# Sixteen projection units as seven block products each, ahead of both attentions, with their results kept in DRAM

## The chip, the cores and the metric

The kernel runs on one core of a Trainium2 chip. The metric is the device time of one execution in microseconds, as the median of several runs. The engines are TensorE (PE in the profile; its weight loads are PEld), VectorE (DVE), ScalarE (ACT), GpSimd (POOL) and SyncE (SP), which issues nearly all DMAs.

## What is computed

One pre-norm layer on x of 1024 tokens x 1024 channels, in float32. Cut to what matters here:

```python
h = rms_norm(x, g)
proj = h @ w_in                    # 1024 x 11280, split into
# c_val, c_gate | g_q, g_k, g_v, g_og, g_f | d_q, d_k, d_v | m_conv, m_gla, m_diff
o_conv = silu(layer_norm(causal_conv31(c_val * sigmoid(c_gate)))) @ w_conv_out
o_gla  = rms_norm(gla(g_q, g_k, g_v, g_f)) * silu(g_og)      # 4 heads, scan over chunks
o_diff = rms_norm(diff_attention(d_q, d_k, d_v)) * 0.8       # 8 heads, two softmaxes each
y = sigmoid(m_conv) * o_conv + sigmoid(m_gla) * o_gla + sigmoid(m_diff) * o_diff
x = x + y @ w_out
x = x + swiglu(rms_norm(x)) @ w_ffn_out                      # FFN of 2816 hidden channels
out = rms_norm(x)
```

## The kernel before

Every float32 matrix product is made of three matmuls in the reduced format: each operand is split into a high and a low half (`hilo`, lines 110 to 112: the cast on ScalarE, the difference on VectorE), and `mm3` (114 to 117) adds high x high, high x low and low x high in PSUM. All weights come as units of 256 output columns (two loads of 512 KB by `raw_half`, four pieces split by `operand`), one unit ahead of their use.

A unit is used by `proj_t` (four outputs of 128 channels x 512 tokens, each over 8 k-tiles: 96 matmuls of 512 columns) or by `proj_n` (tokens on partitions: 192 matmuls of 256 columns, for V and DV). The FFN input product (units FG and FU) is different: it cuts the 256 x 1024 weights and the 1024 x 1024 activations into 2 x 2 blocks and needs seven block products in place of eight (Strassen's scheme in Winograd's form). The block sums of the activations, T1 to T4, are made once; those of the weights (`lefts`, four per unit) and the sums of the products (`copy` on ScalarE, `finish` on VectorE) come in every unit.

`units()` lists the units in order, and the program is written out by a clock of ticks: each `yield` of a projection is a tick, twelve to a unit. On a tick the next weight piece is issued on every second one, convolution taps at a rate of 0.95 per tick (`taps`; each tap is one VectorE instruction over 128 x 1024, `conv_taps`), and every generator that is due (`spawn`, `resume`). For the GLA part the units of a head are CV, A (q and k), V, CV, OG (output gate) and MG (the merge gate); the state scan of the head (`gla_core`, one step for each 128 tokens) and its output (`gla_out`) run among the units that follow. For the attention part they are DV, QK, MD (merge gate), QK for two heads; the softmaxes and value products (`diff_core`) run among the units, spaced by `SPACE` and `LAG` in ticks. Then come MG of the last GLA head, four MC units, the pointwise product PW, the output product WO and the FFN.

Scores lie in PSUM tiles of two banks (`bank2`, two buffers); all else in single banks (`bank`, four buffers). The branch sums lie in y_d in DRAM: the GLA output is stored there, and an attention head loads it, adds its own part on VectorE and stores it again. The framework that builds the program orders the instructions of each engine by its own model of their times, so their order need not be that of the code.

## Time and profile before

| | before |
|---|---|
| median of 3 runs | 2097.28 us (2096.46 to 2097.86) |
| profiled execution | 2096.91 us, span 2095.1 us |
| TensorE busy | 2072.3 us (99%), 10988 matmuls |
| VectorE busy | 1361.4 us (65%) |
| ScalarE busy | 806.3 us (38%) |
| GpSimd busy | 45.5 us (2%) |
| moved by DMA | 196.54 MB, mean 94 GB/s |

The span runs from the first to the last instruction of the profiled execution; its time holds 1.8 us more. A busy share is the union of an engine's instructions; matmuls overlap, so a matmul's own duration is longer than its distance to the next one. In the list of what an engine waited for, the name on the right is the instruction that released it.

### The profile page before, as it was taken

Reading aid. Unit: us, or ns where it says so; the run is one execution under the profiler, and the core shown is the slowest. Engines: PE = TensorE matmul, PEld = TensorE weight load, DVE = VectorE, ACT = ScalarE, POOL = GpSimd, SP = SyncE. Lnnn points to the kernel's source line nnn. Section 1 sums busy time; section 2 is a strip of 40 time slices with the busy share of each in tenths; the row PEclk is TensorE's granted clock in tenths of the full one; section 3 lists DMA queues with packets and bytes.
Section 4 is the critical chain, followed back from the end, with each engine's and each line's share of the span. In section 5 each row is a group of like instructions: output and inputs, shape, how many; then the busy total and the mean of one; then the engine's idle time right before and its main releaser. Section 6 shows DMA issues by size and latency. Waiting matters only on the chain.

```text
span 2095.1 us, 28027 instructions
## 1 busy us (share of the span) xinstructions
PE 2072.3 (99%) x10988; PEld 1779.2 (85%) x10988; DVE 1361.4 (65%) x2056; ACT 806.3 (38%) x1649; POOL 45.5 (2%) x45
## 2 busy tenths in 40 slices
PE   8999999999999999999999999999999999999998
PEld 6988988988898988989888888997888888888886
DVE  5988898798774545545455564469555455577766
ACT  6343252251324545545455451235333333432112
POOL 0000000000000000000000000000000000000000
PEclk9999999999999999999999999999999999999999
DMA  4112112112133323233231555333222222282111
GB/s 161 37 64 77 51 41 81 57 43 72 51 96 86 91 71 106 66 89 92 72 106 61 201 176 170 111 141 119 93 81 98 73 76 96 90 292 89 53 41 81
DMA packets 76579, 196.54 MB, mean 94 GB/s; under 512 B 9024, under 2 KB 19904, under 8 KB 76448
## 3 DMA queue, kind: packets, MB, share of 16 engines
q1 hardware_dynamic: 76448, 194.76, 29.3%
q8 instruction: 86, 1.41, 0.3%
q14 instruction: 45, 0.37, 0.1%
HBM read 137.58 MB, written 38.27 MB: 84 GB/s over the span
## 4 chain that ended last, share of the span: by engine, by line
PE 95%; DVE 3%; issue 1%; POOL 1%; DMA 1%; ACT 0%; SPq 0%; DVEq 0%; POOLq 0%
PE pb L115 23%; PE pb L116 23%; PE pb L117 23%; PE sc L115 6%; PE sc L116 6%; PE sc L117 6%; PE pb L680 3%; PE sc L645 2%; PE sc L644 2%; PE pb L669 2%; POOL sm L122 1%; DVE wl L112 0%; DVE xn L1129 0%; PE pb L504 0%; PE pb L561 0%
## 5 line engine op out<-in xcount | busy, mean ns | idle before, releaser
L115 PE MATMUL pb<-h,wh 128*128 128x512 f32 x1152 | 457.7, 397 | 0.0
L117 PE MATMUL pb<-h,wl 128*128 128x512 f32 x1152 | 450.2, 391 | 0.0
L116 PE MATMUL pb<-h,wh 128*128 128x512 f32 x1152 | 449.9, 391 | 0.0
L111 ACT CAST wh<-wr 128x512 fp32r<-128x512 f32 x331 | 203.7, 622 | 402.5 <-DVE x L1121 139.3
L112 DVE TENSOR_TENSOR wl<-wr,wh 128x512 fp32r<-128x512 f32 x331 | 226.2, 687 | 161.3 <-ACT wh L111 158.5
L362 DVE SCALAR_TENSOR_TENSOR acc<-up,par,acc 128x1024 f32<-128x1024 f32 x240 | 307.0, 1279 | 2.7
L117 PEld LDWEIGHTS pb<-h,wl 128*128 128x128 f32 x1152 | 216.2, 188 | 46.5
L116 PEld LDWEIGHTS pb<-h,wh 128*128 128x128 f32 x1152 | 216.7, 188 | 41.6 <-DVE h L228 0.9
L115 PEld LDWEIGHTS pb<-h,wh 128*128 128x128 f32 x1152 | 216.6, 188 | 41.4 <-ACT h L227 0.3
L1121 DVE TENSOR_TENSOR x<-x,pb 128x512 f32<-128x512 f32 x176 | 120.2, 684 | 61.2 <-PE pb L117 60.6
L115 PE MATMUL pb<-wh,h 128*128 128x256 f32 x512 | 147.8, 289 | 0.0
L117 PE MATMUL pb<-wh,h 128*128 128x256 f32 x512 | 144.9, 283 | 0.0
L116 PE MATMUL pb<-wl,h 128*128 128x256 f32 x512 | 144.8, 283 | 0.0
L115 PE MATMUL sc<-bT,wh 128*128 128x512 f32 x352 | 137.0, 390 | 0.5 <-ACT bT L111 0.5
L116 PE MATMUL pb<-wl,mh 128*128 128x512 f32 x352 | 136.9, 389 | 0.0
L117 PE MATMUL pb<-wh,ml 128*128 128x512 f32 x352 | 136.9, 389 | 0.0
L115 PE MATMUL pb<-wh,mh 128*128 128x512 f32 x352 | 136.9, 389 | 0.0
L116 PE MATMUL sc<-bT,wh 128*128 128x512 f32 x352 | 136.8, 389 | 0.0
L117 PE MATMUL sc<-bT,wl 128*128 128x512 f32 x352 | 136.6, 389 | 0.0
L111 ACT CAST wh<-s 128x512 fp32r<-128x512 f32 x88 | 54.6, 621 | 129.6 <-PE sc L116 91.3
L116 PEld LDWEIGHTS pb<-wl,h 128*128 128x128 f32 x512 | 98.1, 192 | 0.2
L115 PEld LDWEIGHTS pb<-wh,h 128*128 128x128 f32 x512 | 98.1, 192 | 0.2
(242 smaller groups left out, 3663.2 us busy)
## 6 DMA issues: line engine op xcount, KB each, us to landing
wr<-w_dram SPq DMA_DIRECT2D x176, 512.0 KB, 3.7
m_d<-t SPq DMA_DIRECT2D x44, 256.0 KB, 2.1
mr<-m_d SPq DMA_DIRECT2D x22, 512.0 KB, 5.9
y_d<-y SPq DMA_DIRECT2D x28, 256.0 KB, 2.0
k<-k SPq DMA_DIRECT2D x48, 128.0 KB, 2.3
kl<-kl SPq DMA_DIRECT2D x48, 128.0 KB, 2.4
xt<-x_dram SPq DMA_DIRECT2D x8, 512.0 KB, 5.6
c_d<-acc SPq DMA_DIRECT2D x8, 512.0 KB, 2.6
```

Source lines behind the costliest of these rows:

```text
L111: act.copy(hi, src)
L112: vec.tensor_tensor(out=lo, in0=src, in1=f(hi), op=ALU.subtract)
L115: pe.matmul(o, ah, bh, start=start, stop=False, skip_group_check=more)
L116: pe.matmul(o, ah, bl, start=False, stop=False, skip_group_check=more)
L117: pe.matmul(o, al, bh, start=False, stop=stop, skip_group_check=more)
L122: pool.tensor_tensor(out=dst, in0=dst, in1=mhalf[:, 0:width], op=ALU.pow)
L362: vec.scalar_tensor_tensor(out=acc, in0=up[:, j:j + S], scalar=w, in1=acc, op0=ALU.mult, op1=ALU.add)
L644: pe.matmul(sc[i][:, c], a["q"][i][:, t], a["k"][i][:, c], start=True, stop=False)
L645: pe.matmul(sc[i][:, c], a["q"][i][:, t], a["kl"][i][:, c], start=False, stop=True)
L669: pe.transpose(pt[:, i * P:(i + 1) * P], pd[:, (g0 + i) * P:(g0 + i + 1) * P], ident)
L680: pe.matmul(ov[:, 0:P], parts[k // 4][:, c], a["v"][:, k, :], start=k == 0, stop=k == nk - 1)
L1121: vec.tensor_tensor(out=xx, in0=xx, in1=o, op=ALU.add)
```

## The change

Sixteen units (5 CV, 4 OG, 3 MG and 4 MD) move to the front of the list, behind CV 0 and CV 1, and are computed as the FFN input is, by seven block products over all 1024 tokens. The blocks of h are the existing tiles; T1 to T4 are made from them in the head, while CV 0 and CV 1 run. The class `Blocks` is the FFN's loop in a form that both stages use. Their results go to DRAM: the GLU output u to u_d (loaded again for the convolution, one channel tile ahead), the gates of GLA, already multiplied, to gt_d, and those of attention to dg_d; `gla_out` and `diff_core` load them back. The units of a GLA head that remain are A and V, those of two attention heads DV, QK and QK; CV 7 stands ahead of the first GLA head. The pool of the two attentions takes over the SBUF of the block stage when that is done, and the low-rank gate product is made then (`gla_begin`).

The taps have a rate by stage. A state step of GLA comes every two ticks, no longer three; the softmaxes come every two or three. The sums over convolution channels (s_d) and over branches (y_d, heads 0 to 5) are made by accumulating DMAs from GpSimd's queue. The scaling of osb and the factor dng move from VectorE to ScalarE.

```diff
-    out = []
+    out = [("CV", 0), ("CV", 1)]
     for h in range(NH):
-        out += [("CV", 2 * h), ("A", h), ("V", h), ("CV", 2 * h + 1), ("OG", h)]
-        if h < NH - 1:
-            out += [("MG", h)]
+        out += [("OG", h)] + [("MG", h)] * (h < NH - 1) + [("CV", 2 + h), ("MD", h)]
+    out += [("CV", 6)]
+    out += [("CV", 7)]
+    for h in range(NH):
+        out += [("A", h), ("V", h)]
     for j in range(ND // 2):
-        out += [("DV", j), ("QK", 2 * j), ("MD", j), ("QK", 2 * j + 1)]
+        out += [("QK", 2 * j), ("DV", j), ("QK", 2 * j + 1)]
     out += [("MG", NH - 1)] + [("MC", u) for u in range(4)]
...
-LAG = (3, 4, 3, 3, 4, 3, 5, 4)
-SPACE = (2, 2, 2, 3, 3, 4, 3, 3)
-SPACE_LAST = (1, 1, 2, 3, 2, 2, 5, 3)
+
+MIX0, MIX1 = 2, 18
+LAG = (3, 3, 3, 3, 4, 4, 4, 4)
+SPACE = (2, 2, 2, 2, 2, 2, 3, 3)
+TAP_RATE = {"head": 0.0, "blocks": 0.42, "gla": 0.5, "diff": 0.72}
...
+
+    conv = {"ready": deque(), "next": deque(), "now": None, "n": 0}
+    ups = [cv.tile([P, S + 32], F32, name=f"up{i}") for i in range(2)]
+
+    def conv_load():
+        while conv["ready"] and len(conv["next"]) + (conv["now"] is not None) < 2:
+            ct = conv["ready"].popleft()
+            up = ups[conv["n"] % 2]
+            conv["n"] += 1
+            sp.dma_start(up[:, TAPS - 1:TAPS - 1 + S], u_d[ct])
+            conv["next"].append((ct, up))
+
+    def conv_step():
+        if conv["now"] is None:
+            if not conv["next"]:
+                return False
+            conv["now"] = conv_taps(*conv["next"].popleft())
+        if next(conv["now"], None) is None:
+            conv["now"] = None
+        conv_load()
+        return True
+
     def taps(n):
         clock["conv"] = min(clock["conv"] + n, 2.0)
-        while clock["conv"] >= 1.0 and convq:
+        while clock["conv"] >= 1.0 and conv_step():
             clock["conv"] -= 1.0
-            if next(convq[0], None) is None:
...
-        taps(0.95)
+        taps(TAP_RATE.get(clock["stage"], 0.5))
...
+            if full is not None:
+                full[k] = x2_("hf")
+                act.activation(full[k], pt, AF.Copy, scale=g)
...
+        for name in ("T1", "T2", "T3", "T4"):
+            tblock(name)
+        for k in range(4):
+            a, b = full.pop(k), full.pop(k + 4)
+            old = lambda name, p: f(T[name][p][:, k, :])
+            put = lambda name, src: hilo(T[name][0][:, k, :], T[name][1][:, k, :], src)
+            t1, t2 = x2_("t1"), x2_("t2")
+            vec.tensor_tensor(out=t1, in0=a, in1=old("11", 0), op=ALU.subtract)
+            vec.tensor_tensor(out=t1, in0=t1, in1=old("11", 1), op=ALU.subtract)
+            put("T1", t1)
+            vec.tensor_tensor(out=t2, in0=b, in1=t1, op=ALU.subtract)
+            put("T2", t2)
+            yield 1
+            vec.tensor_tensor(out=b, in0=b, in1=a, op=ALU.subtract)
+            put("T3", b)
+            vec.tensor_tensor(out=t2, in0=old("21", 0), in1=t2, op=ALU.subtract)
+            vec.tensor_tensor(out=t2, in0=t2, in1=old("21", 1), op=ALU.add)
+            put("T4", t2)
+            yield 1
+        clock["stage"] = "blocks"
...
-    def conv_taps(ct, up, acc):
+    def conv_taps(ct, up):
+        acc = cv.tile([P, S], F32, tag="acc", name="acc", bufs=1)
...
         sp.dma_start(c_d[ct], acc)
         if ct == 0:
-            vec.tensor_copy(csum, acc)
+            sp.dma_start(s_d, acc)
         else:
-            vec.tensor_tensor(out=csum, in0=csum, in1=acc, op=ALU.add)
-        if ct == KT - 1:
-            sp.dma_start(s_d, csum)
+            pool.dma_start(s_d, acc, accum_op=ALU.add)
+        yield 1
+
+    def conv_in(ct, half, sg, o):
+
+        vec.scalar_tensor_tensor(out=sg, in0=sg, scalar=1.0, in1=o, op0=ALU.add, op1=ALU.mult)
+        sp.dma_start(u_d[ct][:, hs(half)], sg)
+
+    def conv_out(ct):
+        conv["ready"].append(ct)
+        conv_load()
...
+        if h + 1 < NH:
+            spawn(decay(h + 1), 2)
...
+        spawn(gla_core(h), 9)
...
-                yield 3 if pp else 6
+                yield 2
...
+                y = y2("gt")
+                sp.dma_start(y, gt_d[2 * h + v][:, hs(grp)])
+                yield 1
...
-        spawn(diff_core(h), 3)
+        spawn(diff_core(h), (9, 3)[h % 2])
...
-            at += (SPACE if h < ND - 1 else SPACE_LAST)[i]
+            at += SPACE[i]
...
-        vec.tensor_tensor(out=osb, in0=osb, in1=rs.unsqueeze(2).broadcast_to([P, NT, P]), op=ALU.mult)
+        for t in range(NT):
+            act.activation(osb[:, t, :], osb[:, t, :], AF.Copy, scale=rs[:, t:t + 1])
+        gts = [y2("dgate") for _ in range(2)]
+        for half in range(2):
+            sp.dma_start(gts[half], dg_d[h][:, hs(half)])
         yield 2
         for half in range(2):
             pt = bank()
             for t in range(4):
                 pe.transpose(pt[:, t * P:(t + 1) * P], osb[:, half * 4 + t, :], ident)
-            y = y2("y")
-            vec.scalar_tensor_tensor(out=y, in0=a["gate"][:, hs(half)], scalar=1.0, in1=pt, op0=ALU.add, op1=ALU.mult)
+            y = gts[half]
+            act.activation(pt, pt, AF.Copy, scale=dng)
+            vec.scalar_tensor_tensor(out=y, in0=y, scalar=1.0, in1=pt, op0=ALU.add, op1=ALU.mult)
             if h < 6:
-                yg = y2("yg")
-                sp.dma_start(yg, y_d[h, :, hs(half)])
-                vec.scalar_tensor_tensor(out=y, in0=y, scalar=dng, in1=yg, op0=ALU.mult, op1=ALU.add)
+                pool.dma_start(y_d[h][:, hs(half)], y, accum_op=ALU.add)
             else:
-                vec.tensor_scalar(out=y, in0=y, scalar1=dng, scalar2=None, op0=ALU.mult)
-            sp.dma_start(y_d[h, :, hs(half)], y)
+                sp.dma_start(y_d[h][:, hs(half)], y)
...
+    right = ("11", "T1", "T2", "21", "T3", "T4", "22")
+
+    def lefts(alloc, a11, a21, a12, a22):
+        s_ = {0: a11, 3: a12, 5: a22}
+        p = None
+
+        def comb(to, a, b, op):
+            s_[to] = like(alloc("s"), a11)
+            vec.tensor_tensor(out=s_[to], in0=a, in1=b, op=op)
+
+        while True:
+            p = yield operand(s_[p]) if p is not None else None
+            if p == 1:
+                comb(1, a21, a22, ALU.add)
+            elif p == 2:
+                comb(2, s_[1], a11, ALU.subtract)
+            elif p == 4:
+                comb(4, a11, a21, ALU.subtract)
+            elif p == 6:
+                comb(6, a12, s_[2], ALU.subtract)
...
+        def product(self, n, p):
+            if p == 0:
+                ab = bank2()
+                self.chain[n] = {"a": ab[:, 0:HALF], "b": ab[:, HALF:]}
+            ch = self.chain[n]
+            if p == 3:
+                ch["c"] = bank()
+            o = ch["abacaab"[p]]
+            wh, wl = self.made.pop((n, p))
+            bh, bl = self.blocks[right[p]]
+            fresh = p in (0, 1, 3)
+            for k in range(4):
+                kk = slice(k * P, (k + 1) * P)
+                mm3(o, wh[:, kk], wl[:, kk], bh[:, k, :], bl[:, k, :], fresh and k == 0, k == 3, not fresh)
+                if k % 2:
+                    tick()
+
+        def after(self, n, p):
+            ch = self.chain[n]
+            if p == 0:
+                ch["p1"] = self.copy(ch["a"])
+            elif p == 2:
+                ch["u2"] = self.copy(ch["a"])
+            elif p == 3:
+                self.finish(n, 0, 0, ch["p1"], ch["c"])
+            elif p == 4:
+                ch["u3"] = self.copy(ch["a"])
+                self.finish(n, 1, 1, ch["u3"], ch["b"])
+            elif p == 5:
+                self.finish(n, 1, 0, None, ch["a"])
+            elif p == 6:
+                self.finish(n, 0, 1, ch["u2"], ch["b"])
...
+    def mix_sums(n):
+        raws = [raw_half(MIX0 + n, hf) for hf in range(2)]
+        v = [r.rearrange("p (k c n) -> p c k n", k=4, c=2) for r in raws]
+        return lefts(xs2, v[0][:, 0], v[0][:, 1], v[1][:, 0], v[1][:, 1])
...
+    NM = MIX1 - MIX0
+    order = [(0, 0), (0, 3), (0, 1), (0, 2), (0, 4)]
+    for n in range(1, NM):
+        order += [(n, 0), (n - 1, 5), (n - 1, 6)] + [(n, p) for p in range(1, 5)]
+    order += [(NM - 1, 5), (NM - 1, 6)]
+    mb = Blocks(order, order, mix_sums, T, mix_finish, mix_copy)
...
+    w0 = unit()
+    run(conv_half(0, w0, 0))
+    w1 = unit()
+    run(conv_half(1, w1, 0))
+    run(conv_half(0, w0, 1))
+    conv_out(0)
+    for i, _ in enumerate(conv_half(1, w1, 1)):
+        tick()
+        if i % 2:
+            mb.make()
+    conv_out(1)
+    for n, p in order:
+        for _ in range(2):
+            if len(mb.made) < AHEAD:
+                mb.make()
+        mb.product(n, p)
+        if mb.nxt == len(order) and len(mb.made) < 4 and state["n"] == MIX0:
+            state["n"] = MIX1
+            wstart()
+        mb.after(n, p)
+    drain()
+    sx.release()
+    tp.release()
+    mix = tc.alloc_tile_pool(name="mix", bufs=1)
+    clock["stage"] = "gla"
+    spawn(gla_begin(), 0)
...
+    for kind, i in UNITS[MIX1:]:
         if kind not in mixing:
             break
-        if kind == "QK" and i == 1:
-            while convq:
-                taps(1)
+        if kind == "QK":
+            clock["stage"] = "diff"
+        if kind == "MG":
+            while conv_step():
+                pass
```

## Rows read from the trace of the kernel before

**Rows 1.** The page, busy time by engine and the granted clock in 40 slices.

```profile
PE 2072.3 (99%) x10988; PEld 1779.2 (85%) x10988; DVE 1361.4 (65%) x2056; ACT 806.3 (38%) x1649; POOL 45.5 (2%) x45
...
PEclk9999999999999999999999999999999999999999
```

**Rows 2.** Stretches: length, busy us (instructions) of PE, PEld, DVE, ACT, POOL, clock, DMA share.

```profile
50.00:600.00 550.00, 550.00 (x3035) 479.80 (x3034) 470.78 (x559) 195.85 (x373) 16.88 (x8) 1.00 0.18 57
600.00:1170.00 570.00, 570.00 (x3371) 503.14 (x3371) 289.62 (x542) 268.01 (x689) 13.08 (x8) 1.00 0.32 87
...
1440.00:1835.00 395.00, 394.48 (x1722) 321.15 (x1721) 225.00 (x351) 150.41 (x261) 0.00 (x0) 1.00 0.28 92
```

**Rows 3.** What TensorE waited for: us in total, times, longest us.

```profile
PE pb L225 <- DVE xt L287: 10.0, 5, 8.8
```

**Rows 4.** Timeline, TensorE in the pointwise product: start, duration, instruction.

```profile
1230.31 0.39 PE L115 MATMUL pb<-u,wh 128*128 128x512 f32 x1
...
1317.12 0.39 PE L117 MATMUL pb<-u,wl 128*128 128x512 f32 x1
```

**Rows 5.** Groups of instructions by shape: count, busy us, mean ns.

```profile
L362 DVE SCALAR_TENSOR_TENSOR acc<-up,par,acc 128x1024 f32<-128x1024 f32 x240 | 307.0, 1279 | 2.7
L112 DVE TENSOR_TENSOR wl<-s,wh 128x512 fp32r<-128x512 f32 x88 | 59.9, 684 | 25.6 <-ACT wh L111 25.5
L998 DVE TENSOR_TENSOR t<-sc,c 128x512 f32<-128x512 f32 x44 | 30.0, 683 | 2.1 <-PE sc L117 2.1
L953 DVE TENSOR_TENSOR s<-wr 128x512 f32<-128x512 f32 x42 | 28.9, 688 | 20.4 <-DMA wr<-w_dram 20.4
L382 DVE SCALAR_TENSOR_TENSOR up<-sg,pb 128x512 f32<-128x512 f32 x16 | 11.0, 687 | 17.5 <-PE pb L117 17.5
L488 DVE SCALAR_TENSOR_TENSOR gate<-sgm,gate 128x512 f32<-128x512 f32 x12 | 8.2, 680 | 0.0
L111 ACT CAST wh<-s 128x512 fp32r<-128x512 f32 x88 | 54.6, 621 | 129.6 <-PE sc L116 91.3 <-issue 14.5 <-PE pb L116 13.0
L1010 ACT COPY c<-sc 128x512 f32<-128x512 f32 x66 | 38.3, 580 | 11.1 <-PE sc L117 11.1
L348 ACT ACTIVATE sg<-pb 128x512 f32<-128x512 f32 x16 | 9.5, 594 | 54.1 <-PE pb L117 54.1
```

**Rows 6.** Busy time in one stretch of the GLA part (columns as in rows 2).

```profile
200.00:250.00 50.00, 50.00 (x328) 45.91 (x327) 49.52 (x55) 11.60 (x20) 0.00 (x0) 1.00 0.14 41
```

**Rows 7.** Chain that ended last, in order of time: first and fourth GLA head.

```profile
88.35 0.89 PE pb L504 x8
...
523.49 0.89 PE pb L504 x8
```

**Rows 8.** Timeline, one state step of GLA: its update matmul and its low half.

```profile
260.68 0.28 PE L115 MATMUL pb<-vh,knh 128*128 128x256 f32 x1
...
262.90 0.48 DVE L544 SCALAR_TENSOR_TENSOR ws<-zs,dec,ws 128x256 fp32r<-128x256 f32 x1 [1.18 <-ACT ws L543]
```

**Rows 9.** Chain that ended last: the same step of two attention heads, five heads apart.

```profile
666.68 0.89 PE pb L680 x8
...
996.82 0.89 PE pb L680 x8
```

**Rows 10.** DMA issues: count, KB each, median us to landing.

```profile
xt<-x_dram SPq DMA_DIRECT2D x8, 512.0 KB, 5.6
...
c_d<-acc SPq DMA_DIRECT2D x8, 512.0 KB, 2.6
```

**Rows 11.** What VectorE waited for: low halves 1440 to 1835, reciprocals whole span.

```profile
DVE wl L112 <- ACT wh L111: 107.0, 76, 2.1
...
DVE st L655 <- ACT sc L653: 69.7, 60, 2.6
```

**Rows 12.** Timeline, one softmax over 768 keys: first score matmul, last score read.

```profile
799.24 0.48 PE L644 MATMUL sc<-k,q 128*128 128x512 f32 x1
...
804.11 1.02 DVE L658 SCALAR_TENSOR_TENSOR p<-sc,st,p 128x768 f32<-128x768 f32 x1
```

More of the change, by code (lines that the diff above doesn't have):

```diff
@@ L173, in wk @@
         return tuple(p[:, k % 2 * 256 + c.start:k % 2 * 256 + c.stop] for p in w[k // 2])
-    events, clock = [], {"now": 0, "seq": 0, "conv": 0.0}
-    convq = deque()
+    events, clock = [], {"now": 0, "seq": 0, "conv": 0.0, "stage": "head"}
     def spawn(gen, after=0):
@@ L552, in gla_core @@
             yield 1
+        spawn(gla_out(h), 2)
     def gla_out(h):
@@ L611, in diff_v @@
             yield
-    def diff_m(j):
-        w = unit()
-        for c in range(2):
-            gt = g4("dgate")
-            A.setdefault(2 * j + c, {})["gate"] = gt
-            for half in range(2):
-                o = yield from proj_t(w, c, half, hset)
-                sigmoid2(gt[:, hs(half)], o)
-                yield
     def diff_core(h):
@@ new lines, in body, with __init__, make @@
+    class Blocks:
+        def __init__(self, order, makes, sums, blocks, finish, copy):
+            self.order, self.makes, self.nxt = order, makes, 0
+            self.sums, self.blocks, self.finish, self.copy = sums, blocks, finish, copy
+            self.gens, self.made, self.chain = {}, {}, {}
+        def make(self):
+            if self.nxt < len(self.makes):
+                n, p = self.makes[self.nxt]
+                self.nxt += 1
+                if n not in self.gens:
+                    self.gens[n] = self.sums(n)
+                    next(self.gens[n])
+                self.made[n, p] = self.gens[n].send(p)
+        def product(self, n, p):
[12 more added lines that the diff above has]
+                mm3(o, wh[:, kk], wl[:, kk], bh[:, k, :], bl[:, k, :], fresh and k == 0, k == 3, not fresh)
+                if k % 2:
+                    tick()
[14 more added lines that the diff above has]
+                self.finish(n, 0, 1, ch["u2"], ch["b"])
@@ L1046, in load_x3 @@
                 x3[t + i] = x[:, i, :]
+    fb = Blocks(order, makes, ffn_sums, B, finish, copy)
     for _ in range(4):
-        make()
+        fb.make()
     for at, (n, p) in enumerate(order):
```

310 lines of the change are left out of this document (137 added, 173 removed).

## The prediction, made before the change was run

> **What bounds the kernel now.** I read the page's totals first, then the busy time by stage, then what TensorE waited for, then single instructions. TensorE is busy 99% of the span at the full granted clock [rows 1]. By stage [rows 2] it is busy in all of 50 to 1170 us, where the sixteen units of this change now lie (GLA heads to about 600, attention heads after that); VectorE has 471 of 550 us there in the first part and 290 of 570 in the second. Of what TensorE ever waited for, the longest line is the start, 10.0 us [rows 3]; the few other lines are shorter than 2 us each and lie behind 1300. So in the changed stretch the only thing that ends late is TensorE's own list of matmuls, and a change is worth what it takes off that list, less the waits it makes.
>
> A busy TensorE is no proof of a full one, since matmuls overlap: one 128x512 matmul is shown with 390 ns, but the 384 matmuls of the pointwise product start at 1230.31 and the last of them at 1317.12 [rows 4], which is 86.81 / 383 = 0.2267 us from start to start. That is the price I use. The Trainium skill, "TensorE: Matmul & The Clock Gate", section "Back-to-back issue gap", gives about 131 ns for a sustained matmul of 512 columns; at that figure the saving would be, as an estimate, 192 x 0.131 = 25 us and the time 2080. The trace doesn't agree: 383 intervals in a row at 0.2267 us leave it no chance here.
>
> **Part 1: seven products for eight.** A unit of this shape is 8 k-tiles x 4 outputs x 3 matmuls = 96 matmuls of 512 columns; by block products it is 7 x 4 x 3 = 84. Units 2 to 17 are 5 CV, 4 OG, 3 MG and 4 MD: 16 x 12 = 192 matmuls fewer, 192 x 0.2267 = 43.5 us off TensorE. The FFN input runs the same scheme now: 1722 matmuls in 395 us [rows 2] is 0.2294 each, 0.0027 above the steady pace, while half a microsecond is shown as idle. The 1344 matmuls of the new stage at that pace cost 3.6 us back. Bounds 0 and 3.6; I take 3.6, the same loop.
>
> **Part 2: what the blocks cost VectorE and ScalarE.** Durations from [rows 5]. Per unit: 7 low halves and 4 sums at 0.69, 3 finishing additions at 0.68, the GLU product twice in CV at 0.69, the gate merge four times in MG at 0.68. Over 16 units 112 x 0.684 + 64 x 0.688 + 48 x 0.683 + 10 x 0.687 + 12 x 0.680 = 168.5 us. Taps: 224 ticks x 0.42 = 94 steps, of which 31 in 33 are multiplications, 88 x 1.279 = 113 us. Together 281 of the 308 us (1344 x 0.2294) that TensorE needs: 91%. ScalarE: 112 high halves at 0.62, 48 copies at 0.58 and 54 activations at 0.6 = 130 us, 42%. What hides this is that products are made up to seven ahead, 7 x 12 x 0.2267 = 19 us. That VectorE can run so full without TensorE waiting is shown: 200 to 250 us has VectorE at 49.52 and TensorE at 50.00 [rows 6]. Price 0; without cover it is the first rival.
>
> **Part 3: the head.** The low-rank product moves to the GLA stage (32 matmuls, 7 us, on TensorE either way). New are T1 to T4: 4 k-tiles x 10 VectorE instructions x 0.684 = 27.4 us and 16 high halves and 8 extra copies on ScalarE (about 15 us). They lie beside CV 0 and CV 1, 2 x 96 x 0.2267 = 43.5 us of TensorE, and no taps run there any more. Beside them VectorE has the eight low halves of the second half of h (6), four scalings of x (3), the second unit's weights and the first products' (about 7), four GLU products (2.7): some 46 us for 43.5 of cover, and the first T product is third in order. Bounds 0 and 10 (as long as the wait at the start [rows 3]); I take 3, near what is missing.
>
> **Part 4: GLA with A and V only.** A head now repeats every (523.49 - 88.35) / 3 = 145.0 us [rows 7]; without two CV, OG and MG it is 145.0 - 4 x 96 x 0.2267 = 58.0 us. These 24 ticks are 2.42 us each, and a state step comes every two ticks, 4.8 us (now three, 6.6). The state chain from the update matmul to the end of the low half is 260.68 to 263.38, 2.7 us [rows 8], so 2.1 us remain for VectorE's queue, one tap and a low half. VectorE has per head 145.0 x 471/550 = 124 us now, of which taps 79; less four units' weights (11), GLU, gate and csum work (8) 26 are left, plus 24 x 0.5 x 31/33 x 1.279 = 14.4: 40 of 58. Price 0, bounds 0 and 1 us for each of 28 steps.
>
> **Part 5: attention with QK and DV only.** A head repeats every (996.82 - 666.68) / 5 = 66.0 us [rows 9]; without half an MD unit 66.0 - 10.9 = 55.1, in 18 ticks of 3.06. VectorE: 290 x 66.0/570 = 33.5, less MD's two low halves (1.4), the scaling of osb (1.2, now eight ScalarE instructions) and the dng step (1.5, now in ScalarE and the DMA), plus 18 x 0.72 x 31/33 x 1.279 = 15.6 of taps: 45 of 55, 82%. ScalarE rises from 31 to about 33. Price 0; the second rival says where it ends.
>
> **Part 6: DRAM and the accumulating DMAs.** u, gates and dg go out and come back: some 25 MB more over 1000 us, where the DMA engines are busy 18 and 32% [rows 2]. The new loads and stores stand in SP's queue before weight loads, which are a unit ahead. The 19 accumulating DMAs are in POOL's queue, each waiting for a VectorE result; behind them stands the next head's rstd, with most of a head (55 us) to spare. The one accumulator tile is held by two DMAs before the next channel may start; the plain store takes 2.6 us and a load of this size 5.6 [rows 10], no accumulate is shown, and I bound it by 2.6 and twice 5.6. Two empty steps at 0.42 per tick are about 6 us, so at most 5 us of tap delay per channel, off TensorE's path. Price 0. Handing the SBUF of the block stage to the attention pool makes the GLA preparation wait for the last product, under CV 7's 22 us: 0 to 8, I take 2 (a load and a few copies could stick out).
>
> **The sum**, against the profiled execution's 2096.9 (span 2095.1; 0.4 below the median): 2096.9 - 43.5 + 3.6 + 3 + 2 = 2062.
>
> **Rivals.** First, VectorE becomes the pace. Its waits are not in the demand above: in the FFN low halves waited 107 us in 395 for ScalarE's high half [rows 11]; scaled to 308 us and halved that is 42, and 281 + 42 = 323 is 15 us over TensorE's 308. In attention each reciprocal waits for the exponentials, 69.7 us / 8 = 8.7 per head [rows 11], so 45 + 8.7 + 2 for other waits = 55.9 against 55.1, 6 us in eight heads. 2062 + 21 = 2083. For it: these waits are structural. Against: with taps in the queue they are filled, as in 200 to 250.
>
> Second, slower: the score buffers. For 5 key blocks and more a softmax holds both double banks, from its first score matmul to the last read of its scores: 799.24 to 805.13, 5.9 us [rows 12]. The next may begin after 2 ticks, 6.1 us, and needs the second bank 0.8 later: 6.9 us. Two such narrow places in each of 8 heads. If taps and weight halves stretch the chain to 10 us, the 16 places cost (10 - 6.9) x 16 = 50 us and TensorE, in order, gives the time to nobody: 2062 + 50 = 2112. It eats the whole gain from 6.9 + 35/16 = 9.1 us on. At 0.72 taps a tick 1.8 us are added on average, 7.7 us, which costs 13 us at most; so more than twice that would have to fall into the chain. Against it too: narrow places are followed by wide ones.
>
> Third, the change doesn't take the time it says: the 192 matmuls go, but the block loop, head, handover and the state steps stall near their upper bounds (3.6 + 10 + 8 + three quarters of 28 = 43 us): 2096, no change. That all come together speaks against it.
>
> **How the numbers follow.** Forecast 0.75 (2053 to 2075), VectorE as pace 0.13 (2075 to 2092), score buffers 0.08 (2093 to 2115), no change 0.04. Lowest is 2096.9 - 43.5 = 2053 with all costs at nothing; three below it for work that slides into the start's wait. From 2050 to 2088 holds eight in ten. A measurement of this kernel can tell 0.2%, 4 us: faster 0.86, same 0.05, slower 0.09.
>
> **What would show it.** Right: 84 matmuls per mixing unit starting 0.227 to 0.23 us apart, TensorE near 100% in all stages to the MC units, the attention heads 55 to 57 us apart, GLA heads 58 to 60, VectorE 80 to 95% throughout. Part 2 is wrong if low halves release TensorE in the block stage; part 3 if the first T product waits over 10 us; part 4 if ws releases TensorE, part 5 if score matmuls wait for the exponentials or for the p sum. A slower tap or a granted clock below 1 in the mixing stages would make the whole prediction wrong.

## The result, and the profile after

The changed kernel takes 2116.93 us (median of 4 runs, 2115.08 to 2118.91) against 2097.38 us in the same comparison: 1.0094 times as long, 95% interval 1.0076 to 1.0111. The forecast was 2062 with a range of 2050 to 2088. It was wrong, in sign too. The profiled execution has a span of 2113.3 us, 18.2 longer than before.

The page after, busy time by engine (answers [rows 1]):

```profile
PE 2048.8 (97%) x10796; PEld 1751.7 (83%) x10796; DVE 1447.5 (68%) x2218; ACT 892.8 (42%) x1843; POOL 60.8 (3%) x64
```

There are 192 matmuls fewer, as forecast, and TensorE is no longer busy all the time. The stretches of the kernel after: the first two are those of [rows 2], then the head, the blocks, the handover (the block buffers pass to the attention pool, and the low-rank gate product is made), the GLA heads and the attention heads, then two single slices (columns as in [rows 2]):

```profile
50.00:600.00 550.00, 526.55 (x2579) 442.02 (x2579) 500.95 (x641) 227.08 (x409) 12.62 (x9) 0.98 0.30 94
600.00:1170.00 570.00, 561.16 (x3577) 504.56 (x3577) 342.63 (x618) 312.32 (x822) 31.15 (x25) 1.00 0.36 94
...
0.00:60.00 60.00, 39.99 (x184) 32.02 (x185) 39.69 (x79) 35.01 (x61) 4.92 (x12) 0.97 0.36 135
60.00:375.00 315.00, 308.39 (x1333) 250.97 (x1333) 296.57 (x375) 127.19 (x219) 1.94 (x2) 0.99 0.33 106
375.00:430.00 55.00, 47.30 (x198) 36.65 (x197) 44.73 (x48) 18.58 (x28) 0.86 (x1) 0.94 0.37 105
430.00:700.00 270.00, 256.17 (x1642) 233.17 (x1642) 242.76 (x323) 117.48 (x250) 16.67 (x10) 0.97 0.26 80
700.00:1200.00 500.00, 495.85 (x3093) 442.33 (x3092) 255.52 (x507) 283.15 (x755) 25.93 (x22) 1.00 0.38 101
...
225.00:250.00 25.00, 22.10 (x97) 17.72 (x95) 20.44 (x26) 9.15 (x16) 1.07 (x1) 1.00 0.49 145
250.00:275.00 25.00, 24.62 (x101) 20.05 (x101) 23.78 (x29) 10.83 (x19) 0.00 (x0) 0.93 0.22 71
```

Before, TensorE had 550.00 of 550 in the first of these and the clock at 1.00. Now every stage has a hole, and the granted clock is under 1 in all of them but the attention heads.

To put a number on each stage I count what TensorE lost in it: the length of the stretch less the matmuls that start in it, each at its full-rate spacing from start to start, 0.2267 us for 512 columns [rows 4], and 0.175, 0.12 and 0.1115 for 384, 256 and 128 columns, read in the same way where they follow each other without a wait. The kernel before, whose TensorE is busy throughout from 60 us on, shows how exact that is: 0.6, 0.1, 1.2 and 3.4 us in the four later stages.

| stretch, us | lost before | lost after | more |
|---|---|---|---|
| head, 0 to 60 | 15.2 | 25.7 | 10.5 |
| blocks, 60 to 375 | 0.6 | 13.0 | 12.4 |
| handover, 375 to 430 | 0.1 | 10.6 | 10.5 |
| GLA heads, 430 to 700 | 1.2 | 23.1 | 21.9 |
| attention heads, 700 to 1200 | 3.4 | 10.5 | 7.1 |

Together 62.4 us more. The pointwise product, the first stage that the change leaves alone, starts at 1249.1 instead of 1230.3 [rows 4], 18.8 later, and behind it nothing differs (the FFN input still has its 1722 matmuls in 394.5 us). So the work in front of it shrank by 62.4 - 18.8 = 43.6 us, which is the 192 matmuls at 0.2267 us. This is bookkeeping and no second measurement of the saving, since the losses are counted at that same spacing; that the spacing still holds is shown where nothing waits (from 50 to 225 us TensorE loses under 0.6 us in any 25). More than all of the saving was lost again.

What TensorE waited for between 60 and 700 us, the three longest lines (us in total, times, longest us; before there is none in this stretch):

```profile
PE sc L125 <- DVE t L937: 6.6, 2, 3.3
PE pb L466 <- ACT wfx L457: 6.5, 1, 6.5
PE sc L125 <- ACT ah L121: 4.1, 1, 4.1
```

And VectorE, in the same stretch:

```profile
DVE acc L400 <- DMA s_d<-acc: 24.4, 5, 6.7
```

Line 400 is the first tap of a channel. It writes the one accumulator tile, and waits until the accumulating DMA of the previous channel has read it. The DMA issues (KB each, median us to landing; the plain store answers [rows 10]):

```profile
c_d<-acc SPq DMA_DIRECT2D x8, 512.0 KB, 3.1
...
s_d<-acc POOLq DMA_DIRECT2D x7, 512.0 KB, 8.2
```

The timeline at three places, the head, one change of channel, and the handover (start, duration, engine, line, instruction; in brackets the idle time ahead of it and what ended it):

```profile
12.07 2.42 ACT L121 CAST wh<-wr 128x512 fp32r<-128x512 f32 x4 [10.05 <-DMA wr<-w_dram]
14.39 1.05 ACT L323 ACTIVATE junk<-xt 128x1024 f32<-128x1024 f32 x1
...
17.20 1.12 PE L258 MATMUL pb<-cst,xt 128*128 128x128 f32 x4 [17.20 <-DVE sm L131]
...
233.30 1.07 POOL L408 DMA_DIRECT2D s_d<-acc  x1 [202.19 <-DVE acc L402]
237.15 0.69 DVE L122 TENSOR_TENSOR wl<-s,wh 128x512 fp32r<-128x512 f32 x1
241.53 0.75 DVE L400 TENSOR_SCALAR acc<-up,par 128x1024 f32<-128x1024 f32 x1 [3.69 <-DMA s_d<-acc]
...
249.64 0.69 DVE L937 TENSOR_TENSOR t<-sc,c 128x512 f32<-128x512 f32 x1
250.38 0.50 PE L125 MATMUL sc<-T,wh 128*128 128x512 f32 x1 [3.28 <-DVE t L937]
...
251.91 0.63 PE L125 MATMUL sc<-T,wh 128*128 128x512 f32 x1
252.34 0.63 PE L126 MATMUL sc<-T,wh 128*128 128x512 f32 x1
...
408.89 0.33 SPq L449 DMA_DIRECT2D wf<-wf_dram  x1
410.90 0.30 ACT L121 CAST wfx<-wf 128x128 fp32r<-128x128 f32 x1 [9.93 <-DMA wf<-wf_dram]
412.32 9.17 PE L466 MATMUL pb<-h,wfx 128*96 128x512 f32 x32 [6.54 <-ACT wfx L457]
```

Read the middle part first. GpSimd issues the accumulation at 233.30; VectorE comes to the next channel's first tap at 237.84 and stands 3.69 us. It works its queue in order, so the block finish t (line 937) comes only at 249.64, and the matmul that needs its PSUM bank starts 3.28 us late. Soon after, from 251.91 to 255.3 us, eight matmuls start about 0.43 us apart instead of 0.2267.

In the head, ScalarE's first work on data is now the cast of the first weights, for which it waits until 12.07; the squares of x, for which everything waits, stand behind it, and the first transposes start at 17.20 instead of 8.85. At the handover ScalarE waits 9.93 us for wf, whose load could only be issued once the block buffers were given back, and TensorE stands behind it with the low-rank product.

The chain of work that ended last shows the same stall on its way into a GLA head, and the same step of two attention heads, six heads apart (answers [rows 9]):

```profile
460.54 8.90 DMA s_d<-acc
469.52 0.76 DVE acc L400
...
473.39 1.14 DVE t L483
...
475.13 2.54 DVE t L486 x8
...
481.67 0.52 ACT ah L121
482.23 0.58 PE sc L125
...
756.68 0.89 PE pb L722 x8
...
1093.17 0.89 PE pb L722 x8
```

The accumulation holds VectorE to 469.5, the decay of the next head (483, 486) comes after it, ScalarE waits for that, and TensorE for ScalarE's ah: that is the 4.1 us of the list of waits. The attention heads follow each other every (1093.17 - 756.68) / 6 = 56.1 us, near the 55.1 of the forecast.

### The profile page after: what moved, and what is told of

Same layout as the page of the kernel before. It is cut to its first block, busy times and chain, and to the rows that moved or that the text cites. A ratio compares the mean times of both kernels' runs of the same rounds, so it can differ in the third digit from the quotient of the medians.

```text
span 2113.3 us, 28321 instructions
## 1 busy us (share of the span) xinstructions
PE 2048.8 (97%) x10796; PEld 1751.7 (83%) x10796; DVE 1447.5 (68%) x2218; ACT 892.8 (42%) x1843; POOL 60.8 (3%) x64
## 4 chain that ended last, share of the span: by engine, by line
PE 68%; issue 15%; DVE 9%; DMA 3%; ACT 3%; POOL 1%; SPq 0%; DVEq 0%; POOLq 0%; ACTq 0%
PE pb L125 12%; PE pb L126 12%; PE pb L127 12%; PE sc L125 9%; PE sc L126 9%; PE sc L127 9%; DVE acc L402 3%; DMA s_d<-acc 2%; PE pb L722 2%; DVE wl L122 1%; PE sc L686 1%; PE sc L687 1%; POOL rs L132 1%; PE pb L711 1%; POOL sm L132 0%
## 5 line engine op out<-in xcount | busy, mean ns | idle before, releaser
L121 ACT CAST wh<-wr 128x512 fp32r<-128x512 f32 x315 | 193.5, 621 | 397.9 <-DVE x L1259 139.3
L122 DVE TENSOR_TENSOR wl<-wr,wh 128x512 fp32r<-128x512 f32 x315 | 214.0, 689 | 148.7 <-ACT wh L121 147.9
L125 PE MATMUL pb<-h,wh 128*128 128x512 f32 x704 | 281.4, 400 | 2.0 <-DVE h L261 2.0
L127 PE MATMUL pb<-h,wl 128*128 128x512 f32 x704 | 276.1, 392 | 0.0
L126 PE MATMUL pb<-h,wh 128*128 128x512 f32 x704 | 275.7, 392 | 0.0
L121 ACT CAST wh<-s 128x512 fp32r<-128x512 f32 x152 | 94.4, 621 | 229.9 <-PE sc L126 139.8
L127 PEld LDWEIGHTS pb<-h,wl 128*128 128x128 f32 x704 | 132.6, 188 | 29.0
L125 PEld LDWEIGHTS pb<-h,wh 128*128 128x128 f32 x704 | 132.7, 189 | 26.8 <-DVE h L261 2.2
L126 PEld LDWEIGHTS pb<-h,wh 128*128 128x128 f32 x704 | 132.8, 189 | 24.3 <-issue 0.2
L122 DVE TENSOR_TENSOR wl<-s,wh 128x512 fp32r<-128x512 f32 x152 | 104.0, 687 | 28.4 <-ACT wh L121 28.2
L125 PE MATMUL sc<-T,wh 128*128 128x512 f32 x256 | 101.6, 397 | 6.6 <-DVE t L937 6.6
```

The source lines that it names most:

```text
L121: act.copy(hi, src)
L122: vec.tensor_tensor(out=lo, in0=src, in1=f(hi), op=ALU.subtract)
L125: pe.matmul(o, ah, bh, start=start, stop=False, skip_group_check=more)
L126: pe.matmul(o, ah, bl, start=False, stop=False, skip_group_check=more)
L127: pe.matmul(o, al, bh, start=False, stop=stop, skip_group_check=more)
```

## Experiments

The theory: three separate orders of work on in-order queues eat the saving: VectorE behind the accumulating DMA, ScalarE behind the first weights in the head, ScalarE behind wf at the handover. The rivals: VectorE is simply too full (87 to 95% busy in every hundred from 100 to 700 us), or the two-tick steps of the GLA state are too tight. All runs, with the ratio to the kernel before, VectorE's wait for acc, and TensorE's loss by stage (head, blocks, handover, GLA, attention) from the profile:

| kernel | median us | ratio, interval | span us | wait for acc | lost by stage |
|---|---|---|---|---|---|
| before | 2097.4 | 1 | 2095.1 | | 15.2, 0.6, 0.1, 1.2, 3.4 |
| after | 2116.9 | 1.0076 to 1.0111 | 2113.3 | 24.4 | 25.7, 13.0, 10.6, 23.1, 10.5 |
| e1 | 2088.2 | 0.9941 to 0.9974 | 2092.1 | 4.5 | 27.0, 3.5, 7.2, 14.6, 10.3 |
| e2 | 2108.4 | 1.0041 to 1.0071 | 2106.4 | 23.5 | 20.4, 10.3, 11.5, 24.7, 10.2 |
| e3 | 2111.7 | 1.0058 to 1.0088 | 2109.1 | 24.3 | 24.3, 13.7, 8.3, 22.5, 10.4 |
| e4 | 2112.7 | 1.0062 to 1.0092 | 2108.0 | 24.8 | 25.9, 13.7, 10.3, 13.7, 14.8 |
| e5 | 2080.4 | 0.9901 to 0.9930 | 2077.8 | 3.2 | 20.0, 3.7, 6.0, 8.3, 10.5 |
| e6 | 2098.4 | 1.0001 to 1.0019 | 2095.3 | 13.2 | 25.2, 5.1, 9.7, 15.9, 10.2 |
| e7 | 2091.6 | 0.9961 to 0.9983 | 2088.3 | 3.6 | 25.9, 3.3, 5.6, 8.7, 14.9 |
| e8 | 2090.5 | 0.9952 to 0.9978 | 2088.7 | 7.0 | 24.5, 3.3, 6.9, 14.5, 10.2 |
| e9 | 2083.4 | 0.9924 to 0.9949 | 2080.1 | 1.4 | 24.1, 3.7, 2.4, 9.9, 10.3 |
| e10 | 2089.4 | 0.9954 to 0.9978 | 2086.7 | 4.2 | 26.3, 3.5, 4.4, 13.0, 10.1 |
| e11 | 2079.3 | 0.9900 to 0.9930 | 2077.2 | 1.6 | 20.2, 4.2, 2.9, 9.4, 10.6 |
| e12 | 2076.8 | 0.9892 to 0.9925 | 2074.7 | 2.1 | 20.4, 3.7, 2.6, 9.2, 8.5 |

**e1, the accumulator released early.**

```diff
         else:
-            pool.dma_start(s_d, acc, accum_op=ALU.add)
+            for r in (slice(0, 64), slice(64, 128)):
+                pool.dma_start(s_d[r], c_d[ct][r], accum_op=ALU.add, max_dma_last_dim=1024)
```

> One edit to the changed kernel: the sum over channels in s_d is accumulated from the stored copy in c_d (DRAM to DRAM, in two halves) instead of from acc, so acc is free when the plain store of c_d has landed (3.1 us) and not when the accumulating transfer has (8.2 us). Theory A (the slow accumulate holds the one acc buffer, VectorE stops in order and TensorE behind it): VectorE's 24.4 us of waits for s_d<-acc shrink to under 8 us, TensorE's losses at 225-275 and 325-350 us (5.6 and 5.3 us) go, and the time falls from 2117 to 2103-2110 us. Rival B (VectorE is simply full between 75 and 700 us; an earlier acc lets a tap start earlier and something else waits): 2114-2119 us.

Measured 2088.2 us: 28.7 less by the medians, 21.2 by the profiled spans. The profiled execution is the slowest of the four (2093.85 us, mean granted clock 0.994; the fastest took 2086.82 at 0.998), so the medians are nearer to what the edit is worth. What VectorE waited for, and the DMA issues:

```profile
DVE acc L400 <- DMA c_d<-acc: 4.5, 2, 2.8
...
c_d<-acc SPq DMA_DIRECT2D x8, 512.0 KB, 3.4
...
s_d<-c_d POOLq DMA_DIRECT2D x14, 256.0 KB, 4.4
```

Blocks and GLA heads of e1, columns as above:

```profile
60.00:375.00 315.00, 314.85 (x1376) 256.56 (x1375) 306.17 (x386) 131.29 (x225) 3.81 (x4) 1.00 0.33 108
...
430.00:700.00 270.00, 262.76 (x1738) 243.27 (x1737) 238.91 (x317) 121.69 (x264) 22.38 (x16) 0.97 0.30 89
```

Theory A, and more than it asked for, because it had counted only the blocks: losses fell by 9.5 us there, 3.4 at the handover and 8.5 among the GLA heads. Rival B falls: in the blocks VectorE is now busy 306 of 315 us, 97%, more than before the edit, and TensorE 314.85 of 315. In the blocks a full VectorE does not hold TensorE up; a standing one does.

**e2, the order of the head.**

```diff
-    raws0 = [raw_half(0, hf) for hf in range(2)]
     for t in range(4, NT):
         sp.dma_start(xs[t], x_d[t])
...
     for _ in transposed(xs[0:4], *hset, 0, P_MIX):
         pass
+    raws0 = [raw_half(0, hf) for hf in range(2)]
     wfinish()
...
+    vec.tensor_scalar(out=lam[:, 6:7], in0=sm[:, 11:12], scalar1=0.0, scalar2=0.5, op0=ALU.mult, op1=ALU.add)
...
-        vec.tensor_scalar(out=par[:, c0:c0 + n], in0=par[:, c0:c0 + n], scalar1=0.5, ...)
+        vec.tensor_scalar(out=par[:, c0:c0 + n], in0=par[:, c0:c0 + n], scalar1=lam[:, 6:7], ...)
```

(The loads of the mask and of lq move down with raws0, and the third mixing scalar takes lam in the same way.)

> One edit to the changed kernel: ScalarE and VectorE see the token blocks of x before the first weights and before the scaling of par, as in the kernel before (the two first weight loads are issued behind x, the scaling of par is made to depend on the norm of x). Theory A (order in the head: ScalarE stands 10.05 us at wr while x0 has landed at about 4.5 us): the first transposes start at 9-12 us instead of 17.2, TensorE loses 13-19 us before 50 us instead of 25.4, and the time falls from 2117 to 2106-2111 us. Rival B (the weights, now issued last, take the place of x as the wait): first transposes earlier, but the first product with weights no earlier, 2115-2119 us.

Measured 2108.4 us, 8.5 less, in the range of theory A. The first transposes start at 7.09 us and the first product with weights at 19.60 instead of 25.62, but the loss before 60 us fell only to 20.4, short of the 13 to 19 expected:

```profile
17.55 0.62 ACT L121 CAST wh<-wr 128x512 fp32r<-128x512 f32 x1 [3.92 <-DMA wr<-w_dram]
18.07 2.42 ACT L260 ACTIVATE h<-pb,par 128x512 fp32r<-128x512 f32 x4
...
19.60 0.79 PE L125 MATMUL pb<-h,wh 128*128 128x512 f32 x1 [3.24 <-DVE h L261]
```

Theory A holds for the x part. Of rival B it is true that the weights become a wait, but not that the first product comes no earlier: the weights now land last, their cast stands ahead of the casts of the transposed x, and the first product waits for both.

**e3, wf loaded early.**

```diff
+    wf_c = cpool.tile([P, 128], F32, name="wf_c")
...
-        wf = h2("wf", F32)[:, 0:KT * 16].rearrange("p (k n) -> p k n", k=KT)
+        wf = wf_c.rearrange("p (k n) -> p k n", k=KT)
...
-        sp.dma_start(wf, wf_d)
...
+    sp.dma_start(wf_c.rearrange("p (k n) -> p k n", k=KT), wf_d)
     NM = MIX1 - MIX0
```

> One edit to the changed kernel: the 64 KB of wf are loaded into a buffer of their own during the blocks, not after the block buffers are given back. Theory A (at the handover TensorE stands 6.54 us behind ScalarE, which waits 9.93 us for that load): the wait at L466 falls under 2 us, TensorE's loss in 400-425 us falls from 9.6 to 2-4 us, and the time falls from 2117 to 2109-2113 us. Rival B (the copies of wu and the release of the buffers are as late as the load): 2114-2118 us.

Measured 2111.7 us, 5.2 less, in the range of theory A, but its detail missed: the wait at line 466 fell from 6.5 to 4.4 us, not under 2, and the loss of the stage from 10.6 to 8.3. The load was issued in the head, at 12.08 us; what ScalarE waited for next was the release of the block buffers themselves (its timeline; u_d<-t is a store out of a block buffer):

```profile
407.79 0.30 ACT L122 CAST wfx<-wf_c 128x128 fp32r<-128x128 f32 x1 [7.66 <-DMA u_d<-t]
```

**e4, the taps of two channels among the attention heads.**

```diff
+            if ct >= FIRST:
+                w = lat[:, (ct - FIRST) * TAPS + j:(ct - FIRST) * TAPS + j + 1]
...
         rstd(rs, ss, P, 8)
+        if h == H0:
+            one_ = lat[:, (KT - FIRST) * TAPS:]
+            vec.tensor_scalar(out=one_, in0=rs[:, 0:1], scalar1=0.0, scalar2=1.0, op0=ALU.mult, op1=ALU.add)
+            vec.tensor_scalar(out=lat[:, 0:(KT - FIRST) * TAPS], in0=par[:, P_DW + FIRST * TAPS:P_DW + KT * TAPS], scalar1=one_, ...)
+            gate["open"] = True
```

> One edit to the changed kernel: the taps of channels 6 and 7 (62 of 248, 79 us of VectorE) are made to depend on the norm of the first attention head (diff stage), so that they can't be placed among the GLA heads, where VectorE is 93% busy, but run in the diff stage, where it is 50-56% busy. Theory A (VectorE is full in the GLA stage, and its queue delays the casts, scans and state updates for which TensorE waits): TensorE's loss between 425 and 700 us falls from 24 to 8-12 us, the diff stage loses at most 4 us more, and the time falls from 2117 to 2100-2108 us. Rival B (the chains of a GLA head, step by step, set its losses whatever VectorE's load): 2113-2118 us. Rival C (the moved taps cost the attention heads as much as they cost here): 2114-2122 us.

Measured 2112.7 us, 4.2 less: outside theory A's range and just under rival B's. Its GLA and attention heads:

```profile
430.00:700.00 270.00, 261.90 (x1697) 239.57 (x1696) 180.05 (x271) 124.95 (x267) 10.93 (x9) 0.98 0.27 80
700.00:1200.00 500.00, 491.43 (x3061) 437.42 (x3061) 318.58 (x564) 281.33 (x747) 28.50 (x23) 1.00 0.39 104
```

VectorE has 63 us less to do among the GLA heads and TensorE loses 9.4 less there, but 4.3 more among the attention heads. The edit moves two accumulations along with the taps, so it can't tell load from stall; e7 can.

**e7, e1 and e4 together.**

> The edits of e1 and e4 together: acc free early, and the taps of channels 6 and 7 in the diff stage, so that VectorE has 79 us less to do among the GLA heads. Theory A (once acc is free early, VectorE's load itself costs TensorE nothing; the GLA stage's remaining losses are chains within a head): 2085-2091 us, the same as e1. Rival B (a VectorE that is 93% busy still delays the GLA heads): 2077-2083 us.

Measured 2091.6 us, 3.4 above e1, with overlapping intervals, and 0.6 above theory A's range; rival B's 2077 to 2083 is excluded. Again 5.9 us less are lost among the GLA heads and 4.6 more among the attention heads. Where the taps lie moves the loss about, and gives nothing back.

**e6, the accumulation replaced by a plain store on the same queue.**

```diff
+    p_d = dram.tile([KT, P, S], F32, name="p_d")
...
-            pool.dma_start(s_d, acc, accum_op=ALU.add)
+            pool.dma_start(p_d[ct], acc)
```

> The disputed cost by itself: in the changed kernel GpSimd's queue stores acc plainly into a scratch area in place of adding it to s_d (the sum over channels is left out, so the channel norm works with the first channel group's sum alone). Same buffer, same queue, same bytes, no addition. Theory A (the addition makes the transfer slow): it lands in 3-4 us instead of 8.2, VectorE's waits for acc fall from 24.4 to under 8 us, 2086-2096 us. Rival B (GpSimd's queue makes it slow, whatever it does): it lands in 7-9 us, VectorE waits 18-25 us, 2111-2119 us.

Measured 2098.4 us, between the two theories. The kernel leaves the sum over channels out, as e10 does, so both serve for measuring alone. Waits and issues:

```profile
DVE acc L401 <- DMA p_d<-acc: 13.2, 5, 4.9
...
p_d<-acc POOLq DMA_DIRECT2D x7, 512.0 KB, 5.9
```

The same 512 KB take 3.1 to 3.4 us on SyncE's queue, 5.9 on GpSimd's, 8.2 there with the addition (medians, while the other queue's store reads the same tile). Queue and addition each make about half of the excess. It is also a graded dose: with 24.4, 13.2 and 4.5 us of waits for acc the time is 2116.9, 2098.4 and 2088.2.

**e10, no accumulation over channels at all.**

```diff
-        else:
-            pool.dma_start(s_d, acc, accum_op=ALU.add)
```

> The changed kernel with the accumulating transfers into s_d left out for channels 1 to 7 (the channel norm then works with the sum of channel group 0 alone); acc waits only for its plain store. Theory A (their whole cost is that they hold acc): the same as e1, where they run but don't hold it, 2084-2092 us, and VectorE waits 3-8 us for c_d<-acc. Rival B (the traffic and GpSimd's issues cost by themselves too): 2076-2083 us.

Measured 2089.4 us, the same as e1 with its sum from c_d (26.6 us less than the changed kernel by the spans). Theory A: the accumulations cost nothing that can be measured but the hold on acc.

**e8, e1 with the GLA state steps three ticks apart.**

```diff
-                yield 2
+                yield 3
             for p in range(4):
                 act.activation(o4[:, p, :], oo[:, p, :], AF.Square, ...)
```

> The edit of e1, and the steps of the GLA state spaced three program steps apart as in the kernel before, instead of two. Theory A (two steps apart the state chain is on TensorE's path): the waits inside the GLA heads shrink, 2078-2085 us. Rival B (the two-step spacing costs nothing, the losses there lie at the handover between heads): 2086-2092 us.

Measured 2090.5 us, rival B: the spacing costs nothing that can be measured, and the GLA loss stays (14.5 against 14.6).

**e5, the edits of e1, e2 and e3 together.**

> The three edits of the runs e1 (sum accumulated from c_d), e2 (x first in the head) and e3 (wf in a buffer of its own) together. Theory A (three separate losses, each ahead of the next in TensorE's order): their gains add up, 28.7 + 8.5 + 5.2 = 42.4 us, so 2117 falls to 2072-2078 us; the wait that e3 takes out may already be partly gone with e1 (its handover loses 7.1 us, not 9.6), which is the upper end. Rival B (a later stage has a limit of its own that gives the gain back): 2080-2088 us.

Measured 2080.4 us, 36.5 less than the changed kernel, 2 above theory A's range and at the lower edge of rival B's. By the medians the single gains come to 42.4, 6 more than the measured one; by the profiled spans to 21.2 + 6.9 + 4.2 = 32.3, against 35.5. Within that scatter they add up, and no later stage lost more than in e1 by over 0.2 us. What is left lies in the head (20.0 us lost, 15.2 before), at the handover (6.0), and among the heads. The GLA heads lose 8.3 instead of e1's 14.6 though no edit touches them. TensorE's idle time there explains 1.4 of these 6.3 us (7.2 in e1, 5.8 here); most of the rest are matmuls spaced wider: the granted clock of 430 to 700 us is 0.97 in e1's profile and 0.99 in this one. Why it fell more often in e1 is open.

**e9, head and handover once more.** Against e5, the first weights are loaded ahead of x4 to x7 again and their casts take a scale that depends on the norm of x; the low-rank product is placed later:

```diff
+            act.activation(wh, src, AF.Copy, scale=one_)
...
         vec.memset(C["z2"], 0.0)
-        yield 2
+        yield 4
...
         vec.tensor_tensor(out=wu[64:96], in0=wu3[64:96], in1=f(wu[64:96]), op=ALU.subtract)
-        yield 1
+        yield 2
```

> e5 with its two weak places mended: in the head the first weights are loaded as early as in the changed kernel, but their casts, the mask and the scaling of par are made to depend on the norm of x (so that the casts of the transposed x come before them on ScalarE); at the handover the low-rank product is placed three program steps later, behind the first products of CV 7. Theory A (both places are orders of work on an engine's queue, and the work that stood behind them was ready): TensorE's loss before 60 us falls from 20.0 to 15-17 us and in 375-430 us from 6.0 to 2-3 us, so 2080 falls to 2072-2077 us. Rival B (what is moved back at the handover then comes too late for the first GLA head): the loss moves into 430-480 us, 2078-2083 us.

Measured 2083.4 us, 3 above e5, and above the ranges of both theories. The handover did what theory A says: 2.4 us lost instead of 6.0, though the GLA heads lost 1.6 more. The head did the opposite, 24.1 instead of 20.0:

```profile
14.37 1.06 ACT L328 ACTIVATE junk<-xt 128x1024 f32<-128x1024 f32 x1 [3.03 <-DMA xt<-x_dram]
...
18.51 0.29 DVE L377 TENSOR_SCALAR msk<-mskf,lam 128x128 uint8<-128x128 f32 x1 [2.80 <-DMA mskf<-msk_dram]
...
21.36 0.76 PE L126 MATMUL pb<-h,wh 128*128 128x512 f32 x1 [5.79 <-DVE h L266]
```

With the weights out of the way, the squares of the fifth and sixth block of x and the mask took their place in front of the casts that the first product needs.

**e11, the rest of the head put in order.**

```diff
+    vec.tensor_scalar(out=one_h, in0=f(hset[1][0][1][:, 1, 0:1]), scalar1=0.0, scalar2=1.0, op0=ALU.mult, op1=ALU.add)
...
-        act.activation(junks[:, t % 2, :], xs[t], AF.Square, accum_out=ss)
+        act.activation(junks[:, t % 2, :], xs[t], AF.Square, scale=1.0 if t < 4 else lam[:, 6:7], accum_out=ss)
```

> e9 with one more place of the head put in order: the squares of the second half of x, the mask, the mixing scalars and the scaling of par are made to depend on the transposed first half, so that on ScalarE and VectorE they stand behind it, as in the kernel before. In e9 ScalarE stood 3.0 us at the fifth block of x and VectorE 2.8 us at the mask, ahead of the casts for the first product, which began at 21.4 us. Theory A (order of the queues in the head): first product with weights at 16.5-18.5 us, TensorE's loss before 60 us 14-17 us instead of 24.1, time 2073-2078 us. Rival B (the loads themselves are late): first product after 19 us, 2079-2084 us.

Measured 2079.3 us, 4.1 less than e9, in rival B's range. The first product starts a little earlier than expected:

```profile
16.20 0.50 PE L126 MATMUL pb<-h,wh 128*128 128x512 f32 x1
```

But 20.2 us are lost before 60 us, not 14 to 17: TensorE waits 7.2 us for x0 and 2.7 for x1, about the 10.0 of before [rows 3], and 4.9 more later on, for the second half of x and for weights. Theory A holds for the first product and not for the rest of the head.

**e12, the scores of an attention head one step closer.**

```diff
-SPACE = (2, 2, 2, 2, 2, 2, 3, 3)
+SPACE = (2, 1, 2, 2, 2, 2, 3, 3)
```

> e11 with the scores of the blocks 2 to 7 of each attention head one program step earlier (SPACE (2, 1, 2, 2, 2, 2, 3, 3)), which gives the last blocks one step (1.8 us) more before the next head wants their score buffers. Theory A (TensorE's waits of 0.6 us at the first scores of a head are the narrow place of the score buffers): those 7 waits (3.9 us in all) go, 2-5 us less than e11. Rival B (they are taken up by another wait, or the closer start waits within the head): within 1.5 us of e11.

Measured 2076.8 us, 2.5 less than e11 with overlapping intervals, so the time alone doesn't tell. TensorE's waits in this stage fell from 4.1 to 3.0 us and its loss from 10.6 to 8.5: some of the 0.6 us waits went, and others came within the head. The page of this kernel, the fastest here, and its GLA heads:

```profile
PE 2035.6 (98%) x10796; PEld 1743.1 (84%) x10796; DVE 1448.7 (70%) x2220; ACT 888.6 (43%) x1843; POOL 66.7 (3%) x71
```

```profile
430.00:700.00 270.00, 263.21 (x1815) 244.33 (x1814) 238.25 (x327) 126.34 (x280) 22.04 (x16) 1.00 0.33 97
```

It computes what both kernels compute and beats them: 0.991 of the time before, 40 us under the changed kernel.

## Why the prediction was wrong

**Part 1, right.** 192 matmuls went, and where nothing waits the rest keep their spacing, so the saving of 43.5 us is there. The loop's excess of 3.6 was right too: without the stall the blocks lose 3.5 us (e1), against 0.6 before.

**Part 6 failed, and it decided the result.** It saw the one accumulator tile held by two DMAs, and bounded the accumulation by 2.6 and 11.2 us; the trace has 8.2. The size was not the main error, though two of the five stops, 6.0 and 6.7 us, are longer than the 5 it allowed. The error is the phrase "at most 5 us of tap delay per channel, off TensorE's path". The tap that waits is not a spare piece of work beside the others: it stands in VectorE's queue, and the low halves, sums and finishes that TensorE needs stand behind it. There are five such stops, of 3.6 to 6.7 us; those that end at 241.5, 323.1 and 469.5 us are followed by TensorE's waits of 3.3, 3.3 and 4.1 us, so the work made ahead did not cover them. The price was 28.7 us by the medians in e1 (21.2 by the spans) and 27.6 in e10 (26.6); e6 shows it in a middle dose.

The Trainium skill, "DMA: Bandwidth & Descriptors", section "Anatomy of one DMA — SWDGE (gpsimd) path", gives 2.0 us plus the bytes over 436e3 for a transfer from GpSimd's queue, as an estimate 3.2 us for 512 KB. This case doesn't agree: 5.9 plain and 8.2 with the addition; by the Trainium skill's figure the hold would have been as short as in e1.

**Part 6, handover: 2 us (0 to 8) became 10.5.** "Under CV 7's 22 us" was the failing step: the low-rank product stands ahead of most of CV 7 in TensorE's queue. Behind the last block product only 34 matmuls, 397.91 to 405.6 us, come before it, so most of the cover comes after the wait and not beside it. Of the 10.5 us, 3.4 went with the stall at acc (e1). Placing the product three ticks later brought the loss from e5's 6.0 to 2.4 (e9), about the size that was forecast.

**Part 3, the head: 3 us (0 to 10) became 10.5.** It counted VectorE's new work, T1 to T4, and asked whether it fits beside CV 0 and CV 1. It does: from 50 to 225 us under 0.6 us are lost in any 25. What it left out is the order: the casts of the first weights now stand ahead of x on ScalarE. e2, e9 and e11 show that each such order can be changed, and that each edit brings up the next one. In e11 and e12 5 us are left.

**Part 2, right in its price.** VectorE at 97% in the blocks holds nothing up (e1). The first rival, VectorE as the pace, is not what happened. But its load was wrong, here and in parts 4 and 5: by the rates, 88 of the 240 multiplications of the taps were to lie in the blocks, about 45 among the GLA heads and about 97 among the attention heads. In the trace they come earlier (VectorE's time in line 402 by stage, then clock and DMA):

```profile
60.00:375.00 315.00, 143.90 (x113) 0.99 0.33 106
...
430.00:700.00 270.00, 133.11 (x104) 0.97 0.26 80
700.00:1200.00 500.00, 0.15 (x1) 1.00 0.38 101
```

So VectorE is 94% busy in the blocks instead of 91%, 90% among the GLA heads instead of 40 of 58 us, and 51% among the attention heads instead of 82%. A tick is a place in the program and not in the engine's queue, whose order is the framework's.

**Part 4: 0 us (0 to 28) became 21.9.** Of this 8.5 went with the stall at acc (e1). The heads follow each other every 64.2 us, not 58 to 60 (60.1 in e12). The state step, for which the bound was made, costs nothing that can be measured (e8), though ws did release TensorE twice, 1.8 us in all. With all mends (e12) 8.0 us more than before are left: waits of up to 2.1 us for the low halves vl and knl, and shorter ones. That they come from the taps in VectorE's queue is only argued; moving two channels' taps away lowers the loss by 5.9 us and raises the attention heads' by 4.6 (e7).

**Part 5: 0 us became 7.1.** The heads follow every 56.1 us, in the 55 to 57 of the forecast. The second rival's place was right, the score buffers, but its waits are 0.6 us and not 3; at 16 narrow places it gave 50 us, and the trace shows 6 waits, 3.7 us in all. The other 3.4 us are not traced to a cause.

**The third rival** came nearest: block loop, head, handover and GLA near their upper bounds, 43 us in its sum and 55 here. I gave it 0.04, because "that all come together speaks against it". They did not come together by chance: most of the blocks' loss, two fifths of the GLA heads' and a third of the handover's share one cause, the stall at acc.

With the mends, e12's 2076.8 lies 15 above 2062: 8.0 in the GLA heads, 5.1 in the attention heads, and 2.2 more in the head than its term.

## What to carry to other kernels

When an instruction can wait for a transfer, its price is not its own delay but that of everything behind it on its engine, up to the next point where TensorE needs a result; "off the critical path" holds for work, not for a place in a queue. A single buffer read by a slow transfer is such a place: free it with the fast copy and let the slow transfer read that one. And "hidden under the next unit" needs the next unit to stand ahead of the wait in the queue, not behind it.

## What the runs showed of the hardware

A transfer of 512 KB out of SBUF landed after 2.6 us from SyncE's queue in the kernel before and 3.1 in the changed one, after 5.9 from GpSimd's (e6), and after 8.2 when GpSimd's adds to DRAM. From c_d, 256 KB at a time, the addition took 4.4 (e1).

The waits cost more than their length. TensorE's idle time between 60 and 700 us is 28.1 us, its loss 46.7. Part of the difference is the clock: after the 3.28 us of idle before 250.38 eight matmuls from 251.91 on start 0.43 us apart, 1.9 times the full-rate spacing, and the granted clock of 250 to 275 us is 0.93, a mixture of the two levels 2.4 and 1.2 GHz. In the kernel before, TensorE was never idle there and the clock stood at 1.00. So the clock below 1, which the prediction named as a sign against all of it, came here behind waits. Not each wait brought it: a wait of 2.1 us for vl in one GLA head was followed by a slice at 0.93 in e1 and e5 and by none under 1.00 in e12. In the head of e2 the first product, after 3.24 us of idle, starts with 0.43 spacing; in e11, without such a gap, it doesn't.
